# Seven-product form for eight features of the first SwiGLU, with the S5 preparation behind it

## The chip, the core and the metric

The kernel runs on one core of a Trainium2 chip. A core has TensorE (PE, the matrix engine), VectorE (DVE), ScalarE (ACT), GpSimd (POOL) and SyncE (SP), each with its own queue of instructions, and 16 DMA engines that bring data from memory. The metric is the device time of one execution in microseconds (us), the median of several runs. A profile of one further execution shows where the time goes.

## The reference

One decoder layer for 512 tokens of 1024 features, all in float32:

```
h   = x + 1/2 * SwiGLU_1(RMSNorm(x))
u   = RMSNorm(h);  [s5_in | q | k | v | r | a_low | gate_s5 | gate_gla] = u @ W_in
y_s5  = GLU(Re(C . state) + D * s5_in),  state_t = Abar * state_{t-1} + Bbar * s5_in_t
y_gla = (RMSNorm_head(GLA(q, k, v, alpha(a_low)))) * silu(r)
h   = h + W_out( sigmoid(gate_s5) * (y_s5 @ P_s5) + sigmoid(gate_gla) * (y_gla @ P_gla) )
h   = h + 1/2 * SwiGLU_2(RMSNorm(h));  out = RMSNorm_final(h)
SwiGLU(x) = (silu(x @ w1) * (x @ w3)) @ w2,  w1, w3: 1024 x 2816, w2: 2816 x 1024
```

The tables of the S5 branch (powers of its diagonal state matrix, the discretized B and C, the skip term D) depend on parameters alone. The kernel works them out on the chip: this is the S5 preparation.

## The kernel before

Features lie in the 128 partitions, tokens in the free dimension. A float32 product is made from two rounded halves of each operand: `mm3` (lines 229 to 232) issues three matmuls, high by high, high by low, low by high. So each weight tile needs a high half (ScalarE's copy, or a casting DMA from GpSimd) and a low half (VectorE's subtraction, line 87, or ScalarE's negative copy of the high half and then GpSimd's accumulating DMA that adds the weight to it, line 270). A unit whose weights come in the second way is marked `by_dma`.

The program is a list of units, each with the matmuls of about one weight tile. One loop (from line 1775 on) goes through them. For unit n it issues the matmuls, gives back the buffers of unit n-1, starts the load of unit n+5, splits the weights of unit n+3, runs the tasks that are due, then the unit's evacuation (`post`), then the side jobs. So the order of each engine's queue is fixed when the program is written. An engine that waits holds up all that stands behind it in its queue. Buffers come from rings: 5 raw tiles, 6 high, 4 low, and 59 tiles for all else.

The hidden width of a SwiGLU is 22 features of 128. The classic form (`ffn`, and `ffn_seven` for its first features) takes two units for a feature, one for w1 and one for w3, and then `g_post`. The seven-product form (`ffn_seven`, from line 505 on) makes a feature's two projections from seven products of half size, each of 4 x 3 matmuls with 256 columns. The combinations of the inputs are made once (`seven_x`), those of the weights per feature on VectorE. A feature's units have numbers: product 1 needs a half of w1, product 6 the sum s2, and so on. After a group of features come the units of the down projection w2, eight tiles of output. Before, the first SwiGLU is classic (groups of 6, 6, 5 and 5), the second has one classic feature and 21 in the seven-product form.

At the end of the first SwiGLU each output tile is added to h[m] on VectorE; ScalarE squares it and makes the high half of the mixer's input, VectorE makes the low half and gathers the squares (`finish_h`). The mixer's first units are the token-major projections (`wtm`, line 1349 and after); between the third and the fourth stand the small matmuls of the norm (lines 180 and 183).

The S5 preparation (`s5_prep`, a generator) is run as a side job: 56 steps, spread over all units of the first SwiGLU with its last five places left free. Its last part makes tables of powers by doubling: `extend` for 1, 2, 4, 8, 16, 32, 64 with squarings of the phase (`square_phase`) between, all on VectorE, then eight GpSimd instructions (lines 1061 and 1064) that add the skip term to the table `m_t`. The second SwiGLU's entry has its norm factors and its broadcast in the first two units (`at_lead`).

Of the kernel before, what the change touches and what calls it, by code (L numbers as in the profile page):

```python
# [7 lines left out]
F32 = mybir.dt.float32  # L8
# [8 lines left out]
T = 512  # L17
KT = 8
NFF = 22
GROUPS1 = [6, 6, 5, 5]  # L20
# [10 lines left out]
PREP_STEPS = 56  # L31
# [51 lines left out]
def _body(nc, a, sb, pp):  # L83
# [230 lines left out]
    def ffn(w1, w3, w2, groups, norm_key, lead, finish_tile):  # L314
# [14 lines left out]
        c0 = 0  # L329
        for q, nk in enumerate(groups):  # L330
            last = q == len(groups) - 1
            for f in range(c0, c0 + nk):
# [14 lines left out]
                if f == 0:  # L347
                    lead(ua, ub, pa, pb)
# [159 lines left out]
    def ffn_seven(w1, w3, w2, X, groups, classic, norm_key, lead):  # L508
# [4 lines left out]
        def g_post(f, pa, pb):  # L513
            rb = st[norm_key].b
            t1, s, t2 = get(), get(), get()
            mul(t1, pa[0], rb)
            act(s, t1, AF.Silu)
            mul(t2, pb[0], rb)
            mul(t1, t2, s)
            gs[f] = pair()  # L520
            hi_lo(t1, *gs[f])
# [19 lines left out]
        def parts(q, head=2):  # L541
# [5 lines left out]
            def output(m):  # L547
# [6 lines left out]
                def piece(z):  # L554
# [20 lines left out]
                    def post():  # L575
                        if q == len(groups) - 2:
# [21 lines left out]
        def feature(f, final):  # L598
# [47 lines left out]

            def sums_a():
# [20 lines left out]
            def post_2():  # L668
                x = v["x"] = get()
                sub(x[:, left], v["c"][:, left], be)  # L670
                mul(x[:, left], x[:, left], st[norm_key].b[:, left])
                soon(1, lambda: act(x[:, left], x[:, left], AF.Silu, scale=-1.0))
# [49 lines left out]
            def first():  # L722
# [3 lines left out]
                halve(i - 5, "a", ["a11", "a12"], lambda: [w["r1"]])  # L726
# [56 lines left out]
        tail_units(w2, sum(groups[:-1]), groups[-1], gs)  # L783
# [13 lines left out]
    def s5_prep():  # L797
        nonlocal m_t, co_re, co_im
        m_t, co_re, co_im = big(), big(), big()
        G.dma_start(out=s5p, in_=a["s5p"])  # L800
        bc = [get(), get()]
        G.dma_start(out=bc[0], in_=a["s5bc"][:, 0:512])
        G.dma_start(out=bc[1], in_=a["s5bc"][:, 512:1024])
        b_re, b_im = bc[0][:, 0:256], bc[0][:, 256:512]
        c_re, c_im = bc[1][:, 0:256], bc[1][:, 256:512]
        for x in (m_t, co_re, co_im):
            G.memset(x, 0.0)
# [15 lines left out]
        def vexp(x):  # L823
# [4 lines left out]
            ts(n, n, MAGIC, op0=ALU.subtract)  # L828
            stt(y, n, -0.693359375, y, ALU.mult, ALU.add)
            stt(y, n, 2.12194440e-4, y, ALU.mult, ALU.add)  # L830
            ts(p, y, 1.9875691500e-4, 1.3981999507e-3, ALU.mult, ALU.add)
            for c in (8.3334519073e-3, 4.1665795894e-2, 1.6666665459e-1, 5.0000001201e-1):
                mul(p, p, y)
                ts(p, p, c, op0=ALU.add)
            mul(p, p, y)
            mul(p, p, y)
            add(p, p, y)
            ts(p, p, 1.0, op0=ALU.add)
            ts(n1, n, 0.5)
            ts(n1, n1, MAGIC, op0=ALU.add)  # L840
            ts(n1, n1, MAGIC, op0=ALU.subtract)
            sub(n, n, n1)
# [970 lines left out]
```

## Time and profile before

| | us |
|---|---|
| median of 3 runs | 1070.44 (1069.34 to 1070.48) |
| profiled execution | 1068.23 |
| its span | 1066.5 |
| TensorE busy | 1047.9 (98%) |
| VectorE busy | 708.9 (66%) |
| ScalarE busy | 457.4 (43%) |
| GpSimd busy | 137.9 (13%) |

The span goes from the first instruction to the last; the execution's own time lies 1.7 us above it. Times in the rows count from the span's start. The first SwiGLU ends at 377 us, the mixer at about 690, the second SwiGLU fills the rest. In a row, "mm<-g,hi" names the written and the read tiles without their numbers; the square brackets hold the idle time of the engine ahead of the row and who ended it. Line 87 is the helper through which all two-input VectorE instructions go, line 108 the one of all ScalarE instructions.

### The profile page before, as it was taken

To read this page: it belongs to the slowest core of one execution; us is meant where nothing else is said; L and a number is where in the kernel's file an instruction comes from. 1 tells how busy PE (TensorE), PEld (TensorE's weight loads), DVE (VectorE), ACT (ScalarE), POOL (GpSimd) and SP (SyncE) were. 2 spreads that over 40 slices of the span, in tenths; PEclk is the share of its full clock that TensorE was granted. 3 is DMA by queue.
4 is the path that set the end of the run, shared out by engine and by line. 5 is a ranking of instruction groups with operands and counts; after the bars stand their busy time and mean duration, and the time that the engine had idled before them with its cause. 6 is when DMAs were issued, how large, how long until landed. Compare 5 with 4: busy or idle time off the path is not lost.

```text
span 1066.5 us, 15065 instructions
## 1 busy us (share of the span) xinstructions
PE 1047.9 (98%) x5728; PEld 911.3 (85%) x5728; DVE 708.9 (66%) x1484; ACT 457.4 (43%) x846; POOL 137.9 (13%) x222
## 2 busy tenths in 40 slices
PE   9999999999999999999999999999999999999996
PEld 7888888888888898888888888878989999999996
DVE  6688654797644624565364423588998888888966
ACT  7232253322322533553834332664555444544434
POOL 3103600100400122112322222200000000000000
PEclk9999999999999999999999999998999999999998
DMA  7323223322422496477586788712332333233222
GB/s 260 124 60 134 80 83 94 126 85 62 151 84 62 156 234 140 98 163 162 123 190 139 178 197 179 169 34 77 99 125 87 110 109 116 92 100 109 91 69 80
DMA packets 43033, 128.74 MB, mean 121 GB/s; under 512 B 5056, under 2 KB 7552, under 8 KB 42960
## 3 DMA queue, kind: packets, MB, share of 16 engines
q0 software_dynamic: 15456, 55.32, 22.8%
q1 hardware_dynamic: 27072, 71.91, 20.5%
q8 instruction: 45, 0.74, 0.3%
q10 hardware_dynamic: 432, 0.54, 0.1%
q14 instruction: 28, 0.23, 0.1%
HBM read 125.46 MB, written 2.10 MB: 120 GB/s over the span
## 4 chain that ended last, share of the span: by engine, by line
PE 91%; DVE 6%; ACT 1%; issue 1%; DMA 1%; SPq 0%; DVEq 0%; ACTq 0%
PE mm L230 19%; PE mm L231 18%; PE mm L232 18%; PE mm L609 6%; PE mm L612 5%; PE mm L611 5%; PE sp L230 3%; PE sp L231 3%; PE sp L232 3%; DVE g L87 3%; DVE lo L87 1%; ACT g L108 1%; PE sp L1349 1%; PE sp L1350 1%; PE sp L1351 1%; PE mm L1351 1%
## 5 line engine op out<-in xcount | busy, mean ns | idle before, releaser
L230 PE MATMUL mm<-g,hi 128*128 128x512 f32 x848 | 335.6, 396 | 0.0
L231 PE MATMUL mm<-g,hi 128*128 128x512 f32 x848 | 331.5, 391 | 0.0
L232 PE MATMUL mm<-g,lo 128*128 128x512 f32 x848 | 331.1, 390 | 0.0
L108 ACT ACTIVATE g<-g 128x512 f32<-128x512 f32 (+4 forms) x243 | 135.5, 565 | 360.3 <-DVE g L87 345.7
L87 DVE TENSOR_TENSOR g<-g,g 128x256 f32<-128x256 f32 (+8 forms) x416 | 217.2, 537 | 40.0 <-ACT g L108 30.3
L232 PEld LDWEIGHTS mm<-g,lo 128*128 128x128 f32 x848 | 159.2, 188 | 36.5
L230 PEld LDWEIGHTS mm<-g,hi 128*128 128x128 f32 x848 | 159.4, 188 | 33.5
L231 PEld LDWEIGHTS mm<-g,hi 128*128 128x128 f32 x848 | 159.4, 188 | 32.9
L87 DVE TENSOR_TENSOR lo<-raw,hi 128x1024 fp32r<-128x1024 f32 (+3 forms) x124 | 134.9, 1092 | 40.3 <-ACT hi L108 24.2
L108 ACT ACTIVATE hi<-raw 128x1024 fp32r<-128x1024 f32 (+3 forms) x124 | 114.0, 938 | 39.5 <-PE mm L231 33.0
L87 DVE TENSOR_TENSOR g<-mm,g 128x256 f32<-128x256 f32 (+1 forms) x107 | 56.8, 531 | 93.7 <-PE mm L232 71.5
L87 DVE TENSOR_TENSOR g<-g,mm 128x512 f32<-128x512 f32 (+1 forms) x77 | 46.6, 611 | 58.0 <-PE mm L232 54.2
L609 PE MATMUL mm<-b,hi 128*128 128x256 f32 x252 | 71.3, 283 | 4.9 <-ACT g L108 4.9
L609 PE MATMUL mm<-g,hi 128*128 128x256 f32 x252 | 71.5, 284 | 1.3 <-DVE g L87 0.9
L612 PE MATMUL mm<-b,lo 128*128 128x256 f32 x252 | 71.2, 283 | 0.0
L611 PE MATMUL mm<-b,hi 128*128 128x256 f32 x252 | 71.2, 283 | 0.0
L611 PE MATMUL mm<-g,hi 128*128 128x256 f32 x252 | 70.7, 281 | 0.0
L612 PE MATMUL mm<-g,lo 128*128 128x256 f32 x252 | 70.7, 281 | 0.0
L230 PE MATMUL sp<-g,g 128*128 128x512 f32 (+1 forms) x176 | 65.6, 373 | 0.0
L231 PE MATMUL sp<-g,g 128*128 128x512 f32 (+1 forms) x176 | 65.4, 372 | 0.0
L232 PE MATMUL sp<-g,g 128*128 128x512 f32 (+1 forms) x176 | 65.1, 370 | 0.0
L108 ACT ACTIVATE lo<-hi 128x1024 fp32r<-128x1024 f32 x52 | 54.8, 1055 | 20.8 <-PE mm L232 13.4
(192 smaller groups left out, 1528.5 us busy)
## 6 DMA issues: line engine op xcount, KB each, us to landing
hi<-win POOLq DMA_DIRECT2D x24, 512.0 KB, 5.2
lo<-win POOLq DMA_DIRECT2D x24, 512.0 KB, 5.4
raw<-w1a SPq DMA_DIRECT2D x21, 512.0 KB, 3.5
raw<-w3a SPq DMA_DIRECT2D x21, 512.0 KB, 3.6
raw<-w1b SPq DMA_DIRECT2D x21, 512.0 KB, 3.5
raw<-w3b SPq DMA_DIRECT2D x21, 512.0 KB, 3.6
raw<-w2b SPq DMA_DIRECT2D x40, 256.0 KB, 2.7
raw<-w2a SPq DMA_DIRECT2D x16, 384.0 KB, 3.1
```

What stands on the lines that cost most here:

```text
L87: V.tensor_tensor(out=out, in0=x, in1=y, op=op)
L108: S.activation(out, x, f, **kw)
L230: PE.matmul(out, lhsT=wh, rhs=xh, start=start, stop=False)
L231: PE.matmul(out, lhsT=wh, rhs=xl, start=False, stop=False)
L232: PE.matmul(out, lhsT=wl, rhs=xh, start=False, stop=stop)
L609: PE.matmul(bank, lhsT=wh[:, c], rhs=xh, start=start and k == 0, stop=False, skip_group_check=True)
L611: PE.matmul(bank, lhsT=wh[:, c], rhs=xl, start=False, stop=False, skip_group_check=True)
L612: PE.matmul(bank, lhsT=wl[:, c], rhs=xh, start=False, stop=k == 3, skip_group_check=True)
L1349: PE.matmul(banks[i], lhsT=xh, rhs=wh, start=(k == 0), stop=False)
L1350: PE.matmul(banks[i], lhsT=xh, rhs=wl, start=False, stop=False)
L1351: PE.matmul(banks[i], lhsT=xl, rhs=wh, start=False, stop=(k == KT - 1))
```

## The change

The first SwiGLU becomes three parts. Features 0 to 4 are classic; features 5 to 12 take the seven-product form of `ffn_seven`, with the combinations of x made in units 3 to 9; then x is fetched again (`again`), and features 13 to 21 are classic in groups of 5 and 4 (`ffn`). The program has 436 units: the first classic part begins at 0, the seven-product section at 10, the second classic part at 114, the mixer at 148, the second SwiGLU at 199.

The S5 preparation is cut into 73 steps: 22 in the seven-product section, one every third unit from 18 on, and 51 in the second classic part, mostly two per unit, up to its last unit but one in full. Its 64 small copies go from GpSimd to ScalarE, its memsets to VectorE, its last six DMAs to SyncE.

In the seven-product form the halves of w1 come by a casting DMA, a negative ScalarE copy and an accumulating DMA, where the unit lies far enough in (26 features of both SwiGLUs). Units 7 to 9 and the second classic part from its third unit on get their weights by DMA. At the entry of the second SwiGLU the ScalarE table is loaded in its first unit, the norm factors move to its third, the broadcast to its sixth, the classic feature's `g_post` is put off by seven units. In the tail, four instead of three output tiles begin ahead of the last feature.

```diff
-GROUPS1 = [6, 6, 5, 5]
+GROUPS1 = [5, 4, 4]
+GROUPS1_REST = [5, 4]
...
-PREP_STEPS = 56
+PREP_STEPS = 73
+EARLY_STEPS = 22
+X1_STEPS = [(3, 1), (4, 2), (5, 2), (6, 2), (7, 3), (8, 3), (9, 1)]
...
+            for i, do in enumerate((a, b, c, d, e)):
+                soon(behind + i, do) if behind else do()
...
+            def cast():
+                w["hi"] = his.take()
+                G.dma_start(out=w["hi"], in_=w1[f])
+
+            def rest():
+                hh, ll = w["a"] = w["hi"], los.take()
+                for i, k in enumerate(("a11", "a12")):
+                    w[k] = hh[:, i * T:(i + 1) * T], ll[:, i * T:(i + 1) * T]
+                act(ll, hh.bitcast(F32), AF.Copy, scale=-1.0)
+                G.dma_start(out=ll, in_=w1[f], accum_op=ALU.add)
...
-                halve(i - 5, "a", ["a11", "a12"], lambda: [w["r1"]])
+                if i - 13 < opened:
+                    halve(i - 5, "a", ["a11", "a12"], lambda: [w["r1"]])
+                    return
+                fetches.append((i - 13, [his], cast))
+                tasks.append((i - 6, [los], rest))
...
-    f1 = ffn(a["w1a"], a["w3a"], a["w2a"], GROUPS1, "n1", lead1, finish_ffn1)
+    X1 = {}
+    f1 = ffn_seven(a["w1a"], a["w3a"], a["w2a"], X1, GROUPS1, GROUPS1[0], "n1", lead1, 0, again)
     at_lead(f1, "n1", 3)
+    rest1 = len(units)
+    ffn(a["w1a"], a["w3a"], a["w2a"], sum(GROUPS1), GROUPS1_REST, "n1", finish_ffn1)
...
-                        G.tensor_copy(xv[half, :, gg, 3 - j, :], v3(src)[rows, 4 * b:4 * b + 4])
+                        act(xv[half, :, gg, 3 - j, :], v3(src)[rows, 4 * b:4 * b + 4], AF.Copy)
...
-            if m < 3:
+            if m < 4:
                 product(0, m, range(nk - 1))
-                for i in range(3 if m == 2 else 0):
+                for i in range(4 if m == 3 else 0):
...
-    f2 = ffn_seven(a["w1b"], a["w3b"], a["w2b"], X2, GROUPS2, 1, "n2", lead2)
-    at_lead(f2, "n2", 0)
+    f2 = ffn_seven(a["w1b"], a["w3b"], a["w2b"], X2, GROUPS2, 1, "n2", lead2, 7, None)
+    units[f2].post = lambda: act(idle[:, 0:1], idle[:, 0:1], AF.Silu)
+    first_copy = units[f2 + 2].post
+    units[f2 + 2].post = lambda: (first_copy(), st["n2"].factors(spps.get()))
+    units[f2 + 5].post = lambda: st["n2"].finish(spps.get())
...
-    spots = spots[:-5]
-    for k in range(PREP_STEPS):
-        side(spots[k * len(spots) // PREP_STEPS], prep)
+    for k in range(PREP_STEPS - EARLY_STEPS):
+        side(spots[k * len(spots) // (PREP_STEPS - EARLY_STEPS)], prep)
+    for k in range(EARLY_STEPS):
+        side(f1 + 2 * GROUPS1[0] + 8 + 3 * k, prep)
...
+    for u in units[f1 + 7:f1 + 2 * GROUPS1[0]] + units[rest1 + 2:mix0]:
+        u.by_dma = u.split is None
```

Two places show how queues are arranged anew. The first is VectorE at the last down-projection units of the first SwiGLU. The names g_95 to g_102 are h[0] to h[7]; 128x16 rows are a squaring of the phase, 128x256 rows an `extend` by 64. Before:

```order
L87 TENSOR_TENSOR g_100<-g_100,mm_90 128x512
L99 SCALAR_TENSOR_TENSOR g_2841<-g_99,vec,g_2840 128x512
L87 TENSOR_TENSOR g_2753<-g_2753,g_2838 128x512
L87 TENSOR_TENSOR g_101<-g_101,mm_87 128x512
L99 SCALAR_TENSOR_TENSOR g_2867<-g_100,vec,g_2866 128x512
L87 TENSOR_TENSOR g_2753<-g_2753,g_2864 128x512
L87 TENSOR_TENSOR g_102<-g_102,mm_88 128x512
```

In this stretch of VectorE's queue after the change, names as above, between the additions to h[5] and h[6]:

```order
L90 TENSOR_TENSOR g_100<-g_100,mm_90 128x512
L102 SCALAR_TENSOR_TENSOR g_3616<-g_99,vec,g_3615 128x512
L90 TENSOR_TENSOR g_3441<-g_3441,g_3613 128x512
L90 TENSOR_TENSOR g_885<-g_885 128x16 x4
L106 TENSOR_SCALAR g_885<-g_885 128x16
L90 TENSOR_TENSOR g_885<-g_885 128x16 x3
L108 TENSOR_SCALAR g_885<-g_885 128x16
L90 TENSOR_TENSOR g_885<-g_885 128x16 x2
L90 TENSOR_TENSOR g_3288<-g_3567,g_885 128x256
L90 TENSOR_TENSOR g_3289<-g_3568,g_885 128x256
L90 TENSOR_TENSOR g_3567<-g_3288,g_3289 128x4x64
```

Before, the tiles of h follow one another; now a squaring and two extensions by 64 (the second not shown, nor the two that follow it for the next table) stand between two of them.

The second place is GpSimd's queue around the eight instructions of the skip term (written to the big tile b, the table `m_t`). Before:

```order
L994 COPY b_455<-g_864 64x16x16 x2
L999 DMA b_455<-g_864 16x16x16 x2
L999 DMA b_455<-g_864 32x16x16 x2
L999 DMA b_455<-g_864 48x16x16 x2
L1061 TENSOR_TENSOR g_1678<-idn,s5p 128x512
L1064 TENSOR_TENSOR b_455<-b_455,g_1678 128x512
```

GpSimd's queue after the change, with the weights of the mixer's third (lo_76) and fourth (lo_77) units on either side, and two of the eight instructions where they begin and the last two:

```order
L254 DMA hi_72<-win 128x1024
L273 DMA lo_76<-wtm 128x1024
L1141 TENSOR_TENSOR g_3288<-idn,s5p 128x512
L1144 TENSOR_TENSOR b_2427<-b_2427,g_3288 128x512
...
L1141 TENSOR_TENSOR g_3289<-idn,s5p 128x512
L1144 TENSOR_TENSOR b_2427<-b_2427,g_3289 128x512
L254 DMA hi_68<-win 128x1024
L273 DMA lo_77<-wtm 128x1024
L273 DMA lo_74<-win 128x1024
```

Before, the eight stood ahead of all weight DMAs of the mixer; now they stand in the midst of them.

## Rows read from the trace of the kernel before

**Rows 1.** The page: busy time of each engine, share of the span, instructions.
```profile
PE 1047.9 (98%) x5728; PEld 911.3 (85%) x5728; DVE 708.9 (66%) x1484; ACT 457.4 (43%) x846; POOL 137.9 (13%) x222
```

**Rows 2.** TensorE's waits: who waited for whom; us, times, longest.
```profile
PE mm L609 <- ACT g L108: 5.4, 2, 4.9
...
PE mm L230 <- DVE g L87: 0.9, 1, 0.9
```

**Rows 3.** Timeline, 512-column matmuls: start, us, what, count, [idle before].
```profile
689.75 0.39 PE L230 MATMUL mm<-g,hi 128*128 128x512 f32 x1
...
701.88 0.39 PE L232 MATMUL mm<-g,lo 128*128 128x512 f32 x1
```

**Rows 4.** Timeline, TensorE, products of 256 columns.
```profile
825.98 0.28 PE L609 MATMUL mm<-g,hi 128*128 128x256 f32 x1
...
828.81 0.28 PE L609 MATMUL mm<-g,g 128*128 128x256 f32 x1
```

**Rows 5.** TensorE's wait; stretches: length, busy PE, PEld, DVE, ACT, POOL, PEclk, DMA.
```profile
722.36 0.58 PE L609 MATMUL mm<-b,hi 128*128 128x256 f32 x1 [4.91 <-ACT g L108]
...
720.00:725.00 5.00, 2.64 (x12) 2.65 (x13) 4.80 (x9) 2.30 (x6) 0.00 (x0) 0.50 0.20 64
...
725.00:730.00 5.00, 5.00 (x38) 5.00 (x37) 4.54 (x9) 2.75 (x6) 0.00 (x0) 0.83 0.20 61
```

**Rows 6.** Timeline, VectorE: one tile of h in the last down-projection.
```profile
361.22 0.68 DVE L87 TENSOR_TENSOR g<-g,mm 128x512 f32<-128x512 f32 x1
...
362.48 0.69 DVE L87 TENSOR_TENSOR g<-g,g 128x512 f32<-128x512 f32 x1
```

**Rows 7.** Timeline, VectorE: extensions, squaring and copies of the S5 preparation.
```profile
205.37 1.07 DVE L87 TENSOR_TENSOR g<-g,g 128x32 f32<-128x32 f32 x6
...
206.35 0.55 DVE L87 TENSOR_TENSOR g<-g 128x16 f32<-128x16 f32 x4
...
207.83 1.22 DVE L87 TENSOR_TENSOR lo<-raw,hi 128x1024 fp32r<-128x1024 f32 x1
...
218.16 2.46 DVE L87 TENSOR_TENSOR g<-g,g 128x256 f32<-128x256 f32 x6
...
226.59 0.22 DVE L1049 COPY g<-g 128x128 f32<-128x128 f32 x1
...
227.68 1.67 DVE L87 TENSOR_TENSOR g<-g,g 128x128 f32<-128x128 f32 x6
...
275.51 2.47 DVE L87 TENSOR_TENSOR g<-g,g 128x256 f32<-128x256 f32 x6
```

**Rows 8.** Timeline, GpSimd: first and last of eight skip-term instructions.
```profile
278.15 1.46 POOL L1061 TENSOR_TENSOR g<-idn,s5p 128x512 f32<-128x512 f32 x1 [81.42 <-DVE g L87]
...
288.60 2.32 POOL L1064 TENSOR_TENSOR b<-b,g 128x512 f32<-128x512 f32 x1
```

**Rows 9.** Timeline, TensorE: the mixer's first unit, the norm, the fourth unit.
```profile
377.01 0.40 PE L1349 MATMUL sp<-hi,g 128*128 128x512 f32 x1
...
394.16 0.95 PE L180 MATMUL mm<-cst,g 128*128 128x1 f32 x8
...
396.83 0.61 PE L1349 MATMUL sp<-hi,g 128*128 128x512 f32 x1
```

**Rows 10.** DMA issues: KB each, median to landing; GpSimd's issue, mean ns.
```profile
lo<-win POOLq DMA_DIRECT2D x24, 512.0 KB, 5.4
...
lo<-wtm POOLq DMA_DIRECT2D x8, 512.0 KB, 7.2
...
L251 POOL DMA_DIRECT2D hi<-win x24 | 15.9, 663 | 31.7 <-PE mm L232 28.4 <-PE mm L1351 3.3
```

**Rows 11.** Timeline, TensorE and ScalarE: product 6 and the next product 1.
```profile
862.50 0.28 PE L609 MATMUL mm<-b,hi 128*128 128x256 f32 x1
...
870.84 0.28 PE L609 MATMUL mm<-b,hi 128*128 128x256 f32 x1
...
862.56 1.04 ACT L108 ACTIVATE hi<-raw 128x1024 fp32r<-128x1024 f32 x1
```

More of the change, by code (lines that the diff above doesn't have):

```diff
@@ L506, in seven_x, with ffn_seven @@
         yield
-    def ffn_seven(w1, w3, w2, X, groups, classic, norm_key, lead):
+    def ffn_seven(w1, w3, w2, X, groups, classic, norm_key, lead, behind, end):
         gs = {}
@@ L575, in post @@
                     def post():
-                        if q == len(groups) - 2:
+                        if end is None and q == len(groups) - 2:
                             tail_rows(m, box["bank"])
@@ L670, in post_2 @@
                 sub(x[:, left], v["c"][:, left], be)
-                mul(x[:, left], x[:, left], st[norm_key].b[:, left])
-                soon(1, lambda: act(x[:, left], x[:, left], AF.Silu, scale=-1.0))
+                late = 3 if behind and f == classic else 0
+                soon(late + 1, lambda: act(x[:, left], x[:, left], AF.Silu, scale=-1.0))
+                norm = lambda: mul(x[:, left], x[:, left], st[norm_key].b[:, left])
+                soon(late, norm) if late else norm()
             def mm_6():
@@ L782, in ffn_seven, with again, fetch, high @@
             fill = None
-        tail_units(w2, sum(groups[:-1]), groups[-1], gs)
-        return first
-    f1 = ffn(a["w1a"], a["w3a"], a["w2a"], GROUPS1, "n1", lead1, finish_ffn1)
+        if end is None:
+            tail_units(w2, sum(groups[:-1]), groups[-1], gs)
+        else:
+            end()
+            for _ in parts(len(groups) - 1, 4):
+                pass
+        return first
+    def again():
+        due = len(units)
+        def fetch(k, box):
+            box.append(raws.take())
+            for i in range(2):
+                nc.sync.dma_start(out=box[0][:, i * T:(i + 1) * T], in_=a["x"][k + i])
+        def high(k, box):
+            xs[k] = pair()
+            act(xs[k][0], box[0][:, k % 2 * T:(k % 2 + 1) * T], AF.Copy, scale=g1[:, k:k + 1])
+        def low(k, box):
+            stt(xs[k][1], box[0][:, k % 2 * T:(k % 2 + 1) * T], g1[:, k:k + 1], xs[k][0].bitcast(F32), ALU.mult,
+                ALU.subtract)
+            if k % 2:
+                raws.drop(box[0])
+        for k in range(0, KT, 2):
+            box = []
+            fetches.append((due - 6 + 2 * k, [raws], lambda k=k, box=box: fetch(k, box)))
+            for i in range(2):
+                tasks.append((due + 2 + k + i, [], lambda k=k + i, box=box: high(k, box)))
+                tasks.append((due + 3 + k + i, [], lambda k=k + i, box=box: low(k, box)))
+    X1 = {}
+    f1 = ffn_seven(a["w1a"], a["w3a"], a["w2a"], X1, GROUPS1, GROUPS1[0], "n1", lead1, 0, again)
     at_lead(f1, "n1", 3)
+    rest1 = len(units)
+    ffn(a["w1a"], a["w3a"], a["w2a"], sum(GROUPS1), GROUPS1_REST, "n1", finish_ffn1)
     n_ffn1 = len(units)
@@ L834, in vexp @@
                 ts(p, p, c, op0=ALU.add)
+                if c < 0.1 and c > 0.03:
+                    yield
+            yield
             mul(p, p, y)
@@ L848, in vexp @@
             return p
-        dt = vexp(ldt)
+        dt = yield from vexp(ldt)
         yield
@@ L854, in s5_prep @@
         mul(lx, lre, dt)
-        mag = vexp(lx)
+        mag = yield from vexp(lx)
         free.extend([lx, dt])
@@ L891, in s5_prep @@
         add(sn, k, z)
+        yield
         mul(k, cp, e)
@@ L921, in s5_prep @@
         yield
+        bc = [get(), get()]
+        G.dma_start(out=bc[0], in_=a["s5bc"][:, 0:512])
+        G.dma_start(out=bc[1], in_=a["s5bc"][:, 512:1024])
+        b_re, b_im = bc[0][:, 0:256], bc[0][:, 256:512]
+        c_re, c_im = bc[1][:, 0:256], bc[1][:, 256:512]
+        m_t, co_re, co_im = big(), big(), big()
+        for x in (m_t, co_re, co_im):
+            V.memset(x, 0.0)
+            yield
         v3 = lambda ap: ap.rearrange("p (r h) -> p r h", r=16)
@@ L1751, in _body @@
     assert not tasks and not fetches and not soons
-    for gen in (prep, s5, gl, x2):
+    for gen in (prep, s5, gl, x1, x2):
         assert next(gen, done) is done
```

63 lines of the change are left out of this document (36 added, 27 removed).

## The prediction, made before the changed kernel ran

> **What bounds the kernel now.** Start with the page's first part: TensorE is busy 98% of the span [rows 1], so any edit that takes matmuls away shortens the kernel, and any new wait of TensorE lengthens it one to one. Second, who TensorE waited for [rows 2]: the waits are few. The largest, 4.9 of the 5.4 us on ScalarE, is one single hole, the row of 722.36 [rows 5], at the entry of the second SwiGLU; behind it the clock is granted at 0.50 of full speed (the 1.2 GHz level) and then 0.83 in the next stretch. There is no wait worth the name at the seam between the first SwiGLU and the mixer. Third, the pace of TensorE's rows: with 512 columns, 53 intervals from 689.75 to 701.88, so 0.2289 us each [rows 3]; with 256 columns, 24 intervals from 825.98 to 828.81, so 0.1179 us [rows 4]. Last, VectorE's rows inside the S5 preparation and at the end of the first SwiGLU [rows 6, 7]: they tell how much work is handed from one place to another.
>
> **The change part by part.**
>
> *Matmuls.* A classic feature is two units of 8 x 3 matmuls: 48 x 0.2289 = 10.99 us. In the seven-product form it is seven products of 4 x 3 matmuls of 256 columns: 84 x 0.1179 = 9.90. Eight features: **-8.7 us**. The down-projection of these features has the same columns in all, so I cost it at nothing.
>
> *Entry of the second SwiGLU.* The table load is moved ahead, the norm factors two units and the norm's copy five units in, the first product's preparation is no longer queued behind them. What goes is the hole of 4.91 and the clock behind it: in the ten microseconds from 720 TensorE ran 12 matmuls in 2.64 us where 22 fit, and 38 in 5.00 where 42 fit, (10 + 4) x 0.118 = 1.7 [rows 5]. What is late next is the same operand, some 0.4 us behind the last matmul, since VectorE's low half still has to be made. I take **-6.2**, with bounds 0 and -6.6.
>
> *The tail.* Four instead of three pieces are put ahead of the last feature; the one wait there is TensorE's 0.9 on VectorE [rows 2]. I take **-0.5**, bounds 0 and -0.9. ScalarE, 43% busy [rows 1], takes over GpSimd's 64 small copies of the preparation; nobody waits for them, so nothing is charged.
>
> *The seam from the first SwiGLU to the mixer.* Here the order decides. D is the end of TensorE's unit 141, the second of the last eight down-projection units of the first SwiGLU; each has 4 x 3 matmuls of 512 columns, 12 x 0.2289 = 2.75 us, so TensorE could be done with the first SwiGLU at D + 16.5. VectorE adds h[0] and h[1] only at D, and between there and the last instruction of the preparation it now has in its queue: the extensions by 2 (1.07), 4 (some 1.4, between its neighbours), 8 (1.67, the shape of the row of 227.68) and 16 (2.46), five phase squarings of 1.48 (206.35 to 207.83), eight copies of 1.09 together (226.59 to 227.68), four extensions by 32 of 1.67 and four by 64 of 2.47 [rows 7]. That is 6.6 + 7.4 + 1.1 + 6.7 + 9.9 = 31.7 us of preparation. Between them stand the three instructions per tile for h[2] to h[6], 1.95 us each (361.22 to 363.17) [rows 6], and two adds and one low half for the first two tiles, 2.0: 11.7 more. So VectorE reaches the end of the preparation at about D + 43, where TensorE's matmuls need 16.5. Instructions of one engine run in the order of its queue, so nothing hides this: every h[m] waits behind the preparation of the unit before.
>
> Two chains hang on it, and both end in the fourth unit of the mixer, which before began 396.83 - 377.01 = 19.8 us after the first SwiGLU's end [rows 9], that is D + 36.3. (i) h[7] is added at D + 43, its low half is there at D + 45.5; of the first three mixer units, (19.8 - 2.7 for the norm's small matmuls) / 3 = 5.7 us each, the end of the first, two more and the norm remain: 0.7 + 11.4 + 2.7, so D + 60.3, or 62 if the clock stands at half behind the wait, 1.7 as at the other entry. (ii) GpSimd's eight instructions for the skip term wait for the preparation's last result and block GpSimd's queue: from 278.15 to 290.92 they took 12.8 us [rows 8]. Before, they ran 86 us ahead of the mixer. Behind them in the queue now stands the accumulating DMA for the weights of that fourth unit: 43 + 12.8 + 0.7 for the issue ahead of it, and 5.4 to 7.2 until it lands [rows 10], so D + 62 to 64. Both chains say about D + 62. Against D + 36.3: **+26**, with bounds 22 (uncontended GpSimd instructions, the short landing, no clock loss) and 30 (both chains one behind the other in part).
>
> ScalarE's negative copies for the weights by DMA of units 146 to 150 are queued behind its squares of h[m], which wait for VectorE's late adds; those units wait too, but inside the same 26 us.
>
> *Entry of the seven-product form in the first SwiGLU.* VectorE prepares the combinations of x in units 3 to 9. The trace has no such place there; the nearest is the same entry in the second SwiGLU, 4.9 [rows 5], and there a norm stood in the way as well. Bounds 0 and 4.9; I take **+1**, near nothing, since the preparation's steps have left these units and the weights' low halves of units 7 to 9 have gone to DMA.
>
> *The w1 halves by DMA.* For 26 features the low half is made by a negative copy on ScalarE six units ahead and an accumulating DMA from GpSimd instead of one VectorE subtraction. From the start of a unit with product 6 (862.50) to product 1 of the next feature (870.84) are 8.3 us [rows 11]. ScalarE is then in a copy until 863.6, a short one follows, the negative copy of about 1.05 ends at some 864.9; with 5.4 (the median landing of the mixer's accumulates [rows 10]) the weights are there at 870.3, half a microsecond early; with 7.2 they are 1.3 late. Bounds 0 and 26 x 1.3 = 34; I take **+2**, near the median row. VectorE gains 1.2 us a feature, which TensorE doesn't wait for.
>
> At this place two statements of the Trainium skill pull apart. "DMA: Bandwidth & Descriptors", section "Anatomy of one DMA", gives 2.0 us and the bytes over 436 GB/s: 3.2 for 512 KB; an estimate by it leaves the weights 2.7 us early, and the term would be 0. The trace's 5.4 differs, and an accumulate also reads its target. "SBUF — State Buffer", section "SBUF: two separate sides", says that GpSimd cannot write its DMA's descriptors while certain VectorE instructions hold the port that the two share; by it these DMAs, issued from GpSimd beside a busy VectorE, would be late at many features. No row here shows it apart from the longer landing.
>
> *Sum.* The profiled execution took 1068.2 us: - 8.7 - 6.2 - 0.5 + 26 + 1 + 2 = +13.6, so 1081.8. The runs' median, 1070.4, stands 2.2 above the profiled execution; on that footing 1084. I predict **1084 us**.
>
> **Rivals.**
> (a) *The backlog is hidden*: VectorE is ahead of TensorE when it comes to unit 141, or its preparation rows overlap TensorE's units in a way the order doesn't show. For it: before, TensorE has no wait in this place, and VectorE is busy in 66% of the span only [rows 1]. Against it: the add of h[1] waits for the end of unit 141, so no row behind it can begin earlier, and 43 us do not fit in 16.5. Then only the gains count: 1070.4 - 15.4 + 3 = 1058, faster. It turns at a backlog of about 12 us beyond TensorE's own 16.5: below that the gains win.
> (b) *The accumulating DMAs are late at most features*, on top of the seam: + 0.6 to 1.3 for 26 features, so 15 to 34 instead of 2: 1097 to 1116. For it: the longer landing of the wtm rows; against it: the median of the 24 win rows [rows 10].
> (c) *The entry of the second SwiGLU doesn't improve*, because another operand takes the place: the 6.2 go, 1090. For it: the releaser of the hole is one ScalarE row behind a whole queue on two engines; against it: exactly that queue is thinned out.
> (d) *Only one of the seam's two chains is as long as I say*, and GpSimd's instructions don't block: the first chain alone, without the clock, gives 22 to 24: 1081.
>
> **How the numbers follow.** My forecast with (d) has 0.66, (a) 0.11, (b) 0.10, (c) 0.13. With the forecast, terms taken to their nearer bounds (seam 22, entry -6.6) give 1079, to the farther ones (seam 30, first entry 4.9, accumulate 6) 1096. The least that the seam costs, 22, with all gains at their bounds (-16.2) still is +6: 1076. Range 1072 to 1099: it leaves out most of (a) below and half of (b) above. Two measurements of this kernel can be told apart from 0.2% on, some 2.1 us. Faster than that: (a) where the backlog is hidden nearly whole, 0.09; within it: (a) with a backlog that the gains just pay, 0.04; slower: 0.87.
>
> **What would show it.** In the changed profile: TensorE's waits should name, at the end of the first SwiGLU, VectorE (h adds and low halves) and the accumulating DMA, with idle time of some 25 us between the last down-projection units and the mixer's fourth unit; VectorE's timeline there should show unbroken 128x256 and 128x128 rows; GpSimd's first skip-term instruction should wait on VectorE until after TensorE has finished its down-projections' share. The 4.91 hole should be under 1 us and the half clock moved to the new seam. Product 1 of the seven-product features should have no wait in most features. The forecast is wrong if TensorE runs through the seam with less than 12 us idle, or if the same waits show up at every feature.

## The result, and the profile after

The changed kernel takes 1109.41 us (median of 4 runs, 1106.72 to 1110.05) against 1070.05 before (4 runs). The ratio is 1.0364, interval 1.0345 to 1.0382: 39 us slower, where 14 were forecast and 29 was the upper end of the range. The direction was right, the size was not. (The kernel before has one more run here than when the prediction was made.)

The page's first part, after, answers to [rows 1]. The span is 1107.5 us.

```profile
PE 1054.3 (95%) x6016; PEld 925.0 (84%) x6016; DVE 731.3 (66%) x1624; ACT 515.2 (47%) x1044; POOL 185.1 (17%) x263
```

There are fewer columns to multiply, yet TensorE is busy 6 us longer: part of its work ran at the lower clock (the granted clock of the stretches stands further down). Who TensorE waited for (us in total, times, longest) answers to [rows 2]:

```profile
PE mm L627 <- DMA lo<-w1b: 15.3, 12, 3.5
PE sp L1430 <- DMA lo<-wtm: 10.9, 2, 7.5
PE mm L235 <- DMA lo<-w2a: 7.9, 4, 5.7
...
PE sp L233 <- ACT g L111: 2.2, 1, 2.2
...
PE mm L627 <- DMA lo<-w1a: 1.6, 2, 0.9
```

The 4.9 us hole at the second SwiGLU's entry has gone. Two new kinds of wait have come: at the seam to the mixer (lo<-wtm, lo<-w2a) and inside the seven-product features (lo<-w1b, lo<-w1a). All of them end with an accumulating DMA.

To see what each place costs, I took all intervals between the starts of successive matmuls, less the median interval of the same kind of matmul. An interval more than 0.25 us above it counts as idle, the rest as slow clock. In us:

| place | before: idle, slow | after: idle, slow | difference | forecast |
|---|---|---|---|---|
| first us, to 60 | 2.6, 2.2 | 2.3, 2.0 | -0.5 | |
| entry of the seven-product form, 60 to 85 | 0, 0 | 4.8, 0.3 | +5.1 | +1 |
| first SwiGLU, 85 to 260 | 0, 0.5 | 0.9, 0.1 | +0.5 | part of +2 |
| first SwiGLU's end and the seam, 260 to 430 (before to 420) | 0, 2.2 | 21.4, 8.6 | +27.8 | +26 |
| mixer | 0, 2.7 | 0, 2.8 | +0.1 | |
| entry of the second SwiGLU | 5.3, 1.8 | 3.3, 0.4 | -3.4 | -6.2 |
| features of the second SwiGLU | 1.7, 0.3 | 16.4, 5.6 | +20.0 | part of +2 |
| tail | 4.4, 0.7 | 4.4, 0.6 | -0.1 | -0.5 |

The sum of the differences is 49.5; less the 8.7 of saved matmuls that is 40.8, and the spans differ by 41.0. So the seam cost what was forecast, and the features of the second SwiGLU cost what I had not given them.

The seam first. VectorE's timeline after, from the additions to h[0] and h[1] to h[7] (start, length, what; here D = 357.2, where unit 141 ended):

```profile
357.16 1.37 DVE L90 TENSOR_TENSOR g<-g,mm 128x512 f32<-128x512 f32 x2 [1.93 <-PE mm L235]
...
359.83 1.07 DVE L90 TENSOR_TENSOR g<-g,g 128x32 f32<-128x32 f32 x6
...
373.80 0.68 DVE L90 TENSOR_TENSOR g<-g,mm 128x512 f32<-128x512 f32 x1
...
376.75 3.37 DVE L90 TENSOR_TENSOR g<-g,g 128x128 f32<-128x128 f32 x12
...
394.06 0.74 DVE L102 SCALAR_TENSOR_TENSOR g<-g,vec,g 128x512 fp32r<-128x512 f32 x1
394.72 5.58 DVE L90 TENSOR_TENSOR g<-g,g 128x512 f32<-128x512 f32 x13
400.21 0.68 DVE L90 TENSOR_TENSOR g<-g,mm 128x512 f32<-128x512 f32 x1
400.81 1.23 DVE L102 SCALAR_TENSOR_TENSOR g<-g,vec,g 128x512 fp32r<-128x512 f32 x1
401.96 1.78 DVE L90 TENSOR_TENSOR g<-g,g 128x512 f32<-128x512 f32 x1
403.67 1.52 DVE L102 SCALAR_TENSOR_TENSOR g<-g,vec,g 128x512 fp32r<-128x512 f32 x1
```

The rows of [rows 7] stand here without a break between the additions; h[7] is added at 400.21, D + 43.0, as worked out, and its low half is there at 405.19 (the last row), D + 48.0. ScalarE waits for the addition at 373.80 (that of h[3]) before it squares the tile, and the negative copy for the weights of a later unit stands behind:

```profile
374.57 0.63 ACT L111 ACTIVATE g<-g 128x512 f32<-128x512 f32 x1 [7.06 <-DVE g L90]
...
375.72 0.61 ACT L111 ACTIVATE lo<-hi 128x512 fp32r<-128x512 f32 x1
```

GpSimd's timeline of the same stretch has the accumulating DMA that waits for this copy, and answers to [rows 8]:

```profile
376.63 0.86 POOL L273 DMA_DIRECT2D lo<-w2a  x1 [7.41 <-ACT lo L111]
...
400.44 1.04 POOL L1141 TENSOR_TENSOR g<-idn,s5p 128x512 f32<-128x512 f32 x1 [2.92 <-DVE g L90]
...
410.21 1.27 POOL L1144 TENSOR_TENSOR b<-b,g 128x512 f32<-128x512 f32 x1
...
412.01 0.91 POOL L273 DMA_DIRECT2D lo<-wtm  x1
```

And TensorE's rows that waited there answer to [rows 9]:

```profile
380.93 0.79 PE L235 MATMUL mm<-g,lo 128*128 128x512 f32 x1 [5.65 <-DMA lo<-w2a]
...
388.51 0.81 PE L1430 MATMUL sp<-lo,g 128*128 128x512 f32 x1 [3.40 <-DMA lo<-wtm]
...
410.71 0.61 PE L1429 MATMUL sp<-hi,g 128*128 128x512 f32 x1
418.82 0.81 PE L1430 MATMUL sp<-lo,g 128*128 128x512 f32 x1 [7.50 <-DMA lo<-wtm]
```

The fourth mixer unit begins at 410.71 (D + 53.5) and gets the low half of its weights at 418.8, D + 61.6; the forecast said D + 62. Between 388.51 and 411.3 TensorE has no wait, and none of its waits at the seam ends with VectorE. The four stretches that matter, in the view by windows (columns as in [rows 5]; in order the first entry, the seam, the second entry and the features):

```profile
60.00:85.00 25.00, 20.98 (x128) 18.10 (x127) 23.23 (x48) 14.91 (x32) 4.49 (x10) 1.00 0.42 122
370.00:430.00 60.00, 42.38 (x153) 36.25 (x153) 38.09 (x114) 16.49 (x30) 21.14 (x23) 0.77 0.56 133
740.00:760.00 20.00, 18.35 (x144) 17.21 (x142) 18.35 (x41) 11.24 (x24) 1.41 (x2) 1.00 0.33 83
760.00:1060.00 300.00, 284.83 (x1971) 266.13 (x1972) 228.99 (x439) 131.85 (x282) 24.82 (x35) 0.98 0.56 161
```

Now one late feature of the second SwiGLU, over all engines that have a part in it. TensorE, with the idle time ahead of product 1's third matmul:

```profile
777.41 0.58 PE L627 MATMUL mm<-b,lo 128*128 128x256 f32 x1 [3.47 <-DMA lo<-w1b]
```

ScalarE's negative copy (the row written lo<-hi), six units ahead in the program, and what stands before it:

```profile
768.03 1.04 ACT L111 ACTIVATE hi<-raw 128x1024 fp32r<-128x1024 f32 x1
768.98 0.29 ACT L111 ACTIVATE g<-raw 128x128 fp32r<-128x128 f32 x1
769.18 1.04 ACT L111 ACTIVATE lo<-hi 128x1024 fp32r<-128x1024 f32 x1
```

GpSimd's two issues, and SyncE's two beside them:

```profile
770.51 0.85 POOL L671 DMA_DIRECT2D lo<-w1b  x1 [13.41 <-ACT g L111]
771.06 0.87 POOL L664 DMA_DIRECT2D hi<-w1b  x1
```

```profile
770.70 0.33 SPq L567 DMA_DIRECT2D raw<-w2b  x1
771.12 0.38 SPq L635 DMA_DIRECT2D raw<-w1b  x1
```

The sixth unit ahead began at 767.29 and product 1 at 773.54. The lead is the time from the start of the sixth unit ahead to product 1's third matmul as it would have come without the wait (773.78): 6.5 us here. Of it 3.2 went until the issue, and 6.85 passed until the landing. All 19 such features of the second SwiGLU, by their lead:

| lead, us | issue behind the sixth unit's start, us | landing, us | features | late by, us |
|---|---|---|---|---|
| 6.5 (down-projection pieces of one column between the products) | 3.2 | 5.9, 6.85 | 2 | 3.6, 2.7 |
| 7.9 | 4.4 | 6.6 | 1 | 3.2 |
| 8.6 | 2.65 | 6.3 to 7.65 | 8 | 0.4 to 1.8, 6.4 together |
| 8.5 | 1.6 | 6.3 to 6.35 | 3 | 0 |
| 8.6 | 3.1 to 3.2 | 5.2 to 5.45 | 4 | 0 |
| 10.1 (the first) | 6.1 | 5.3 | 1 | 1.35 |

So with one and the same lead of 8.5 to 8.6 us eight features are late and seven are not: the issue and the landing decide.

### The profile page after: what moved, and what is told of

The parts are those of the page before. It is cut to its first block, busy times and chain, and to the rows that moved or that the text cites. A ratio compares the mean times of both kernels' runs of the same rounds, so it can differ in the third digit from the quotient of the medians.

```text
span 1107.5 us, 16097 instructions
## 1 busy us (share of the span) xinstructions
PE 1054.3 (95%) x6016; PEld 925.0 (84%) x6016; DVE 731.3 (66%) x1624; ACT 515.2 (47%) x1044; POOL 185.1 (17%) x263
## 3 DMA queue, kind: packets, MB, share of 16 engines
q1 hardware_dynamic: 27504, 59.52, 16.4%
## 4 chain that ended last, share of the span: by engine, by line
PE 49%; issue 29%; DVE 8%; DMA 6%; POOL 4%; ACT 2%; SPq 0%; POOLq 0%; DVEq 0%; ACTq 0%
PE mm L233 10%; PE mm L235 10%; PE mm L234 9%; DVE g L90 6%; DMA lo<-w1b 3%; PE mm L627 3%; PE mm L624 2%; PE mm L626 2%; PE sp L233 2%; PE sp L234 2%; PE sp L235 2%; ACT g L111 1%; DMA lo<-w1a 1%; POOL hi L664 1%; DVE g L102 1%
## 5 line engine op out<-in xcount | busy, mean ns | idle before, releaser
L111 ACT ACTIVATE g<-g 128x512 fp32r<-128x512 f32 (+5 forms) x340 | 162.3, 490 | 330.4 <-DVE g L90 308.8
L90 DVE TENSOR_TENSOR g<-g,g 128x512 f32<-128x512 f32 (+5 forms) x474 | 243.3, 529 | 39.8 <-ACT g L111 29.2
L235 PE MATMUL mm<-g,lo 128*128 128x512 f32 x616 | 241.9, 393 | 7.9 <-DMA lo<-w2a 7.9
L233 PE MATMUL mm<-g,hi 128*128 128x512 f32 x616 | 244.8, 397 | 0.1
L234 PE MATMUL mm<-g,hi 128*128 128x512 f32 x616 | 241.3, 392 | 0.0
L233 PEld LDWEIGHTS mm<-g,hi 128*128 128x128 f32 x616 | 116.2, 189 | 24.5 <-DVE g L90 0.5
L234 PEld LDWEIGHTS mm<-g,hi 128*128 128x128 f32 x616 | 116.1, 188 | 23.9
L111 ACT ACTIVATE lo<-hi 128x1024 fp32r<-128x1024 f32 (+2 forms) x113 | 112.5, 1000 | 40.5 <-PE mm L235 27.4
L233 PE MATMUL sp<-g,g 128*128 128x512 f32 (+1 forms) x280 | 106.5, 380 | 2.2 <-ACT g L111 2.2
L234 PE MATMUL sp<-g,g 128*128 128x512 f32 (+1 forms) x280 | 106.1, 379 | 0.2 <-DVE g L90 0.2
L235 PE MATMUL sp<-g,g 128*128 128x512 f32 (+1 forms) x280 | 105.6, 377 | 0.0
L624 PE MATMUL mm<-g,hi 128*128 128x256 f32 x348 | 98.8, 284 | 1.2 <-DVE g L90 1.0
L624 PE MATMUL mm<-b,hi 128*128 128x256 f32 x348 | 98.9, 284 | 0.9 <-ACT g L111 0.9
L626 PE MATMUL mm<-b,hi 128*128 128x256 f32 x348 | 98.5, 283 | 0.0
L626 PE MATMUL mm<-g,hi 128*128 128x256 f32 x348 | 98.4, 283 | 0.0
L627 PEld LDWEIGHTS mm<-b,lo 128*128 128x128 f32 x348 | 67.6, 194 | 20.2 <-DMA lo<-w1b 17.8
```

Of the source, the lines that this page charges most:

```text
L90: V.tensor_tensor(out=out, in0=x, in1=y, op=op)
L111: S.activation(out, x, f, **kw)
L233: PE.matmul(out, lhsT=wh, rhs=xh, start=start, stop=False)
L234: PE.matmul(out, lhsT=wh, rhs=xl, start=False, stop=False)
L235: PE.matmul(out, lhsT=wl, rhs=xh, start=False, stop=stop)
L624: PE.matmul(bank, lhsT=wh[:, c], rhs=xh, start=start and k == 0, stop=False, skip_group_check=True)
```

## The experiments

Eleven kernels. Seven edits start from the changed kernel, three build on those, and one starts from the kernel before. The first four were to price the two big losses.

**e1: w1's low half on VectorE again.**

```diff
-                if i - 13 < opened:
+                if True:
                     halve(i - 5, "a", ["a11", "a12"], lambda: [w["r1"]])
                     return
```

> The changed kernel, but the low half of w1 in every seven-product feature is again made by VectorE from the raw tile (no casting and no accumulating DMA for it). Theory: TensorE's waits for the accumulating DMA (15.3 us on w1b and 1.6 on w1a in the changed profile) and the half clock behind them are the part of the loss that I had put at 2; without them 1109.4 - 21 = about 1088 (1085 to 1092), and TensorE waits less than 2 us inside the seven-product features. Rival: VectorE, with one more subtraction of 1.2 us per feature, becomes late instead; then TensorE waits for VectorE in the same features and the time stays above 1100.

Measured: 1090.67 us (2 runs), 18.7 less than the changed kernel. The waits for lo<-w1b and lo<-w1a are gone; idle and slow time in the features of the second SwiGLU are about 2 instead of 22. VectorE does not become the bound: the 19 us hang on the halves of w1 that come by DMA.

**e2: the accumulate eight units ahead.**

```diff
-                tasks.append((i - 6, [los], rest))
+                tasks.append((i - 8, [los], rest))
```

> The changed kernel with the negative copy and the accumulating DMA of w1 due eight units ahead of product 1 instead of six. Theory: the DMA is late because six units are too short a lead (6.5 to 8.6 us at the late features, against 2.65 until the issue and 6.3 to 7.7 to landing); two units more, 2.1 to 2.8 us, remove the waits of up to 1.9 and leave some 1 of the longest three: about 1092 (1088 to 1097). Rival: the ring of four low tiles has no room earlier, or the transfer is bound by traffic, so that the landing stays where it was: 1105 or more.

Measured: 1084.25 us (2 runs), 25 less, more than the theory gave. One wait of 0.8 us for lo<-w1b is left, and the features lose 0.9 us in all. The DMA was late because it began too late for its landing; two units are enough. I had not counted the half clock behind every wait. The landing also became shorter, so this run changed the lead and the landing together. The view by line of w1's accumulates, minimum, median and maximum, in the changed kernel and in e2:

```profile
DMA to landing us min/median/max: 5.2/6.3/7.6
```

```profile
DMA to landing us min/median/max: 5.2/5.5/6.8
```

**e3: the preparation spread evenly over units 114 to 140.**

```diff
+    spots = list(range(rest1, mix0 - 7))
     for k in range(PREP_STEPS - EARLY_STEPS):
```

> The changed kernel with the 51 late steps of the S5 preparation spread over all units from 114 to 140, none in the last seven units of the first SwiGLU. Theory: the seam's 25 us are VectorE's 31 us of preparation between the additions to h, and GpSimd's skip term behind it; moved ahead, both are hidden: 1109.4 - 25 = about 1084 (1081 to 1089), and VectorE is done with h[7] within 4 us of TensorE's end of the first SwiGLU. Rival: the steps only crowd the units before, where the down projection of the group of 5 has 3.4 us per unit and two steps take about 5; then TensorE waits in units 125 to 140 and the time stays above 1095.

Measured: 1114.32 us (2 runs), 5 more than the changed kernel. The theory's number fell and the rival's held. TensorE waits 11.3 us where it waited 5.7 and 7.5, and another 6.1 ahead of that:

```profile
367.50 0.79 PE L233 MATMUL mm<-g,hi 128*128 128x512 f32 x1 [6.13 <-ACT g L111]
...
389.93 0.79 PE L235 MATMUL mm<-g,lo 128*128 128x512 f32 x1 [11.28 <-DMA lo<-w2a]
```

VectorE's timeline of e3 just ahead shows why:

```profile
309.17 0.69 DVE L90 TENSOR_TENSOR g<-g,mm 128x512 f32<-128x512 f32 x1 [4.58 <-PE mm L235]
316.59 0.69 DVE L90 TENSOR_TENSOR g<-mm,g 128x512 f32<-128x512 f32 x1 [6.74 <-PE mm L235]
322.99 0.69 DVE L102 SCALAR_TENSOR_TENSOR g<-mm,g 128x512 f32<-128x512 f32 x1 [5.71 <-PE mm L235]
```

VectorE is idle most of the time from 300 to 325, since many steps hold only ScalarE copies, and then has the 15 heavy steps together again. Steps were spread, work was not.

**e4: GpSimd's skip term four units into the mixer.** The last step is cut in two, and its second part is run at the end of the mixer's fourth unit.

```diff
+        yield
         for b in range(4):
             w0 = pad[b % 2]
...
+    side(mix0 + 3, prep)
```

> The changed kernel with GpSimd's eight skip-term instructions issued four units into the mixer, behind the weight DMAs of its first units; VectorE's preparation stays where it was. Theory: the last wait of the seam, 7.9 us before the mixer's fourth unit, is GpSimd's block alone (chain ii), and VectorE's lateness (chain i) ends earlier: 1109.4 - 8 = about 1101 (1098 to 1103). Rival, as I had it in the forecast: both chains are of one length, so that VectorE's chain takes over: 1107 or more.

Measured: 1103.40 us (2 runs), 6.0 less, short of the forecast by 2. At the seam TensorE still waits for lo<-w2a and lo<-wtm:

```profile
PE mm L235 <- DMA lo<-w2a: 7.7, 3, 5.6
PE sp L1431 <- DMA lo<-wtm: 3.8, 2, 2.8
```

The 7.5 us wait was GpSimd's block; both chains were not of one length. The waits ahead of it stay, since VectorE's additions are as late as before. VectorE's rows at the end of this chain, h[6]'s gathering addition and h[7]'s low half, now without GpSimd's tensor instructions beside them:

```profile
402.36 0.69 DVE L90 TENSOR_TENSOR g<-g,g 128x512 f32<-128x512 f32 x1
403.15 0.75 DVE L102 SCALAR_TENSOR_TENSOR g<-g,vec,g 128x512 fp32r<-128x512 f32 x1
```

**e5: the preparation spread by its work, accumulate eight units ahead.**

```diff
+    late = [n for n in range(rest1, rest1 + 12) for _ in range(3)] + list(range(rest1 + 12, mix0 - 7))
+    for n in late:
+        side(n, prep)
```

> The changed kernel with w1's accumulating DMA eight units ahead (as in the run before), and the 51 late preparation steps placed by their VectorE work: three per unit in units 114 to 125 (the 36 steps that are mostly ScalarE copies and small products), one per unit in 126 to 140 (the 15 steps of the doubling). Theory: the run with an even spread failed because its heavy steps still lay together in units 133 to 140 while VectorE had stood idle before them for 25 us; spread by work, VectorE is done before unit 141 and the seam costs nothing: 1084.3 - 25 = about 1060 (1057 to 1064). Rival: the preparation has no room in the second classic part at all, the wait only moves ahead again: 1075 or more.

The accumulate is due as in e2. Measured: 1079.90 us (4 runs), ratio to before 1.0090 (1.0075 to 1.0105): 4 less than e2, not 25. VectorE is in time now, but GpSimd's skip term is only moved ahead, into the weight DMAs of the down projection. GpSimd's timeline in e5, and the matmul that waits:

```profile
363.40 1.04 POOL L1141 TENSOR_TENSOR g<-idn,s5p 128x512 f32<-128x512 f32 x1
...
373.27 1.59 POOL L1144 TENSOR_TENSOR b<-b,g 128x512 f32<-128x512 f32 x1
...
375.39 0.92 POOL L273 DMA_DIRECT2D lo<-w2a  x1
...
379.85 0.79 PE L235 MATMUL mm<-g,lo 128*128 128x512 f32 x1 [9.24 <-DMA lo<-w2a]
```

**e6: the high half of w1 by ScalarE, no casting DMA.**

```diff
-                G.dma_start(out=w["hi"], in_=w1[f])
+                act(w["hi"], w["r1"], AF.Copy)
...
-                fetches.append((i - 13, [his], cast))
+                tasks.append((i - 7, [his], cast))
```

> The changed kernel with the high half of w1 in the seven-product form made by ScalarE from the raw tile (seven units ahead) instead of by a casting DMA; the accumulating DMA stays six units ahead. Theory: the accumulate lands in 6.3 to 7.7 us instead of 5.2 because the next feature's casting DMA is issued 0.55 us behind it on the same queue; without that it lands in about 5.3, the waits of the eight features with 8.6 us of lead vanish, and 2 us each remain at the three with a shorter lead: 1109.4 - 14 = about 1095 (1092 to 1098). Rival: SyncE's raw fetches or something else lengthens the landing; it stays above 6 us and the time above 1103.

Measured: 1144.44 us (2 runs), 35 more. The theory fell, the rival held. ScalarE's extra copy puts the negative copy a microsecond back, and the landing became longer without any casting DMA (the view by line of w1's accumulates in e6):

```profile
DMA to landing us min/median/max: 5.1/7.0/9.0
```

The grouping tells it. In e6, five of the 19 accumulates of w1b have no fetch of SyncE in flight and land in 5.2 to 5.5 us; of the 14 others 13 take 6.5 to 9.0. In the changed kernel five have none and land in 5.2 to 5.45, with a casting DMA 0.55 us behind; the 14 others take 5.9 to 7.6. So the landing goes with SyncE's fetches and not with the casting DMA; this is a grouping, and no run moved the fetches alone.

**e7: the entry of the second SwiGLU alone, in the kernel before** (the entry's hunks of the change, nothing else).

```diff
-    f2 = ffn_seven(a["w1b"], a["w3b"], a["w2b"], X2, GROUPS2, 1, "n2", lead2)
-    at_lead(f2, "n2", 0)
+    f2 = ffn_seven(a["w1b"], a["w3b"], a["w2b"], X2, GROUPS2, 1, "n2", lead2, 7)
+    units[f2].post = lambda: act(idle[:, 0:1], idle[:, 0:1], AF.Silu)
...
```

> The kernel before with the edits at the second SwiGLU's entry alone (table load ahead, norm factors, broadcast and classic feature put off, one step of the combinations moved). Theory: 2.3 us of idle and slow clock remain of 7.1 there, as the run with the earlier accumulate shows: 1070.3 - 4.8 = about 1065.5 (1064 to 1067). Rival: what was measured there hangs on the first SwiGLU's new form, and alone the edits bring the 6.2 of the forecast (1064 or less) or nothing (1069 or more).

Measured: 1065.34 us (5 runs), ratio 0.9959 (0.9945 to 0.9973). That is 4.6 gained, as expected; the entry loses 2.8 us instead of 7.1. TensorE's remaining waits there in e7 are small:

```profile
732.11 0.39 PE L624 MATMUL mm<-g,hi 128*128 128x256 f32 x1 [1.05 <-DVE g L87]
734.24 0.38 PE L624 MATMUL mm<-g,hi 128*128 128x256 f32 x1 [0.45 <-ACT g L108]
```

The rows that end these two waits read out a product (the tile mm), VectorE's and ScalarE's:

```profile
731.64 0.41 DVE L87 TENSOR_TENSOR g<-mm,g 128x256 f32<-128x256 f32 x1
...
733.82 0.36 ACT L108 ACTIVATE g<-mm 128x256 f32<-128x256 f32 x1
```

**e8: e5 with the combinations of x one unit earlier.**

```diff
-X1_STEPS = [(3, 1), (4, 2), (5, 2), (6, 2), (7, 3), (8, 3), (9, 1)]
+X1_STEPS = [(2, 1), (3, 2), (4, 2), (5, 2), (6, 2), (7, 3), (8, 2)]
```

> The run with the spread preparation and the accumulate eight units ahead, with the combinations of x made one unit earlier (units 2 to 8 instead of 3 to 9). Theory: the 5 us lost at the entry of the seven-product form in the first SwiGLU come from VectorE, which has the last combinations in its queue ahead of the last classic feature's evacuation; a unit earlier takes away most of the wait of 2.2 on ScalarE and the clock behind: 2 to 4 us below that run. Rival: VectorE is full from unit 2 on, and the same work earlier delays the classic features by as much: within 1 us of that run.

Measured: 1078.35 us (4 runs), 1.6 less than e5, between the two. The loss from 60 to 85 us falls from 4.4 to 1.4, and 1.3 of it comes back ahead of 60.

**e9: e8 with the skip term on VectorE**, two instructions in each of the mixer's first four units.

```diff
         for b in range(4):
+            yield
             w0 = pad[b % 2]
-            G.tensor_tensor(out=w0.rearrange("p (r c) -> p r c", r=4), in0=idn[:, None, :].to_broadcast([P, 4, P]),
+            V.tensor_tensor(out=w0.rearrange("p (r c) -> p r c", r=4), in0=idn[:, None, :].to_broadcast([P, 4, P]),
...
+    for k in range(4):
+        side(mix0 + k, prep)
```

> The last run (preparation spread by its VectorE work, accumulate eight units ahead, combinations of x one unit earlier) with the eight skip-term instructions given to VectorE, two in each of the mixer's first four units. Theory: what was left at the seam, one wait of 9.2 us for an accumulating DMA of w2 and the half clock behind it, is GpSimd's queue, blocked for 11 us by the skip term in the midst of the weight DMAs; without it 1078.4 - 9 - 3 = about 1066 (1064 to 1069), faster than the kernel before. Rival: the accumulates of w2 are late by themselves (ScalarE's negative copies stand behind squares that wait for VectorE); then 1073 or more.

Measured: 1067.07 us (8 runs), ratio 0.9978 (0.9968 to 0.9988), 11 less than e8, as the theory has it. With VectorE in time and GpSimd free, the seam's waits are down to 1.1 us for lo<-w2a and 0.6 for lo<-wtm.

**e10: e9 with a gentler spread.**

```diff
-    late = [n for n in range(rest1, rest1 + 12) for _ in range(3)] + list(range(rest1 + 12, mix0 - 7))
+    late = [n for n in range(rest1, rest1 + 6) for _ in range(3)] + [n for n in range(rest1 + 6, rest1 + 15) for _ in range(2)]
+    late = sorted(late + list(range(rest1 + 15, mix0 - 7)) + [rest1 + 18, rest1 + 20, rest1 + 22])
```

> The run e9 with the first 36 late preparation steps placed three per unit in units 114 to 119 and two per unit in 120 to 128, the 15 doubling steps in 129 to 140. Theory: the waits of 2.2 us (a transpose of the preparation on TensorE for ScalarE) and of 1.4 to 2.3 us (weights behind crowded ScalarE) in units 114 to 125 come from three steps per unit; fewer give 2 to 4 us back: about 1063. Rival: the doubling now starts three units later and VectorE is late again at the end of the first SwiGLU: e9 plus 3 or more.

Measured: 1062.79 us (5 runs), ratio to before 0.9934 (0.9922 to 0.9947): about 1063 as the theory has it, faster than both kernels, and 2.5 faster than the entry's edits alone. The page of e10 (its span is 1061.2 us):

```profile
PE 1038.1 (98%) x6016; PEld 915.3 (86%) x6016; DVE 730.8 (69%) x1632; ACT 516.7 (49%) x1044; POOL 174.2 (16%) x255
```

TensorE is busy 9.8 us less than before, about the 8.7 of the saved matmuls and the clock at the second entry.

**e11: SyncE's fetches one unit later.**

```diff
-                    fetches.append((max(i - 10, opened), [raws], lambda name=name, src=src: fetch(name, src[f])))
+                    fetches.append((max(i - 9, opened), [raws], lambda name=name, src=src: fetch(name, src[f])))
...
-                        fetches.append((max(i - 12, opened), [raws], fetch))
+                        fetches.append((max(i - 11, opened), [raws], fetch))
```

> The changed kernel with SyncE's raw fetches of w1, w3 and w2 inside the seven-product form due one unit later (nine and eleven units ahead instead of ten and twelve); the accumulating DMA stays six units ahead, with the next casting DMA 0.55 us behind it. Theory, formed from the runs before: an accumulate lands in 5.2 to 5.9 us unless SyncE issues a raw fetch within the first microsecond behind it, then in 6.3 to 7.7; shifted by a unit, the fetches come 1.4 to 2 us behind and most landings fall under 5.9, so the waits of 0.5 to 1.8 us at the eight features with 8.6 us of lead go, and about 1 us each at the three short ones: 1109.4 - 12 = about 1097 (1094 to 1101). Rival: the casting DMA on the same queue lengthens the landing; it stays at 6.3 or more and the time at 1107 or more.

Measured: 1112.09 us (2 runs), and a median landing of 6.3 us as in the changed kernel. It decides nothing: in the second SwiGLU SyncE's issues stand where they stood, 0.2 to 1 us behind the accumulate, since the raw buffers come free no earlier and hold the fetches back. That the fetches lengthen the landing therefore rests on the grouping in e6 and in the changed kernel, and on e2, where they come mostly 1.8 us and more behind the issue; no run moved them alone.

## Why the forecast was wrong in its size

*The matmuls* (-8.7): right by the closing sum of the table, and by e10's busy time.

*The seam* (+26): the size is right, +25.4 from 370 on and 2.4 ahead of it. VectorE's backlog of 43 us, GpSimd's block (11.0 instead of 12.8) and the fourth unit's low half at D + 61.6 came as worked out in chain (ii). Chain (i) was wrong, and that it gave the same D + 62 was luck. It let the first of the mixer's units wait for h[7]; but in the kernel (`tm_units`) each of these units takes two tiles of h only, k = 2 * piece + kk, so h[7] is wanted first in the fourth unit. TensorE came there at D + 53.5, when the low half of h[7] had been ready for 5.5 us. The sign that its waits would name VectorE failed. VectorE's late additions reached TensorE another way, which I had put "inside the same 26 us": through ScalarE's squares, the negative copies behind them and the DMAs behind these, in the waits of 5.65 and 3.40 us. e4 shows that GpSimd's chain was the longer, by 6 us of time.

*The w1 halves by DMA* (+2): **this is the step that failed.** It cost 20.0 in the second SwiGLU and 0.5 to 1 in the first, between the bounds 0 and 34 but far from the value that I took. The words were that the weights "are there at 870.3, half a microsecond early". Three things were wrong in them. The landing of 5.4 was the median in the mixer [rows 10]; with SyncE's fetches in flight it is 5.9 to 7.65 here. That alone makes eight features late, which have the lead of [rows 11]: 2.65 us until the issue and 6.3 to 7.65 until the landing are more than 8.6. Next, the lead of 8.3 us to product 1 was read at one feature. It holds for 15 of 19, but three have 6.5 to 7.9, because the down projection's pieces between their products are one column wide; these three hold 9.5 of the 16.4 us of idle time, the eight others 6.4. And the half clock behind the waits, 5 us over all, was not counted. e2 shows it from the other side: two units more of lead, with a median landing of 5.5, take 25 us away. How much of this the lead does alone, and how much the shorter landing, no run shows. My rival (b) had the mechanism, and 1097 to 1116 held the result, but I gave it 0.10, and let the range end where the accumulate cost 6.

Of the two statements of the Trainium skill that I set against each other there, the second is taken up in the last section. By the first, in "DMA: Bandwidth & Descriptors", section "Anatomy of one DMA", 512 KB take an estimated 3.2 us; no accumulate of w1 landed in under 5.1, so the trace differs. The same page of the Trainium skill, section "Issuing engines are not separate DMA queues", says that transfers of all issuing engines share the same 16 DMA engines and interleave; the landings of 5.2 to 5.45 without and 5.9 to 7.6 beside SyncE's fetches agree.

*The first entry* (+1): it was 5.1, just beyond my bounds. The wait of 2.2 on ScalarE is the last classic feature, behind the combinations of x in VectorE's queue; e8 moves them and takes 3.0 of it away there.

*The second entry* (-6.2): -3.4 in the changed kernel, where feature 1's late accumulate took 1.2 back, and -4.6 alone (e7). The hole went, but what is late next is not the operand that I named, VectorE's low half: in e7 the larger waits of 0.45 and 1.05 us end with the rows in which ScalarE and VectorE read out a product. VectorE's rows go there without a gap from 720.78 on, so its read-out comes when its queue has got to it.

*The tail* (-0.5): nothing; the wait of 0.9 is there as before.

Rival (a), that the backlog is hidden, is refuted by the timeline of VectorE; (c) by e7. Rival (d) was right that one chain alone had the length, but it was GpSimd's, and GpSimd's instructions do block (e4, e9).

## What to carry to other kernels

A lead given in units is not a time: before a transfer is tied to "six units ahead", list the shortest six units in the program and set them against the longest landing beside the other traffic of that place, not one pair of rows against a median from elsewhere. When side work is spread over a program, spread each engine's time, not the steps, and ask of each engine that also issues DMAs what stands behind the side work in its queue. A new form that saves 1% on the bound engine pays only when all its feeders are in time at every seam; the edit that paid here by itself was the one that thinned a queue.

## What the runs showed of the hardware

VectorE's rows at the seam grew beside GpSimd's skip-term instructions: the gathering addition of 401.96 took 1.78 us and the low halves of 400.81 and 403.67 took 1.23 and 1.52, where the same forms take 0.69 [rows 6] and 0.74 (394.06). In e4, where GpSimd's tensor instructions come later, the same rows take 0.69 and 0.75 again. GpSimd's own went between 1.04 and 1.49, and 1.27 and 1.62. The Trainium skill, "SBUF — State Buffer", section "SBUF: two separate sides", says that VectorE and GpSimd share a port that one of them holds for a whole instruction; the rows agree with it. That the accumulating DMAs are delayed by this port, which I had from the same page, no run shows: they land in 5.2 us beside a VectorE that is busy 76% of the features' stretch.

A wait of TensorE costs more than itself: in the stretch of the seam the granted clock is 0.77, and the slow matmuls add 7.8 us to 19.8 of idle time, most of them behind its four waits (about 2 of the 7.8 are there in the kernel before, too). In the features 16.4 us of idle time bring 5.6.
